# Products of ones ahead of the data, a first weight unit in halves, the first norm's squares on ScalarE and TensorE, and the last weight unit by token tile, in a two-layer mixer encoder

## The chip, the cores and the metric

The kernel runs as one program on one core of a Trainium2 chip. The metric is the device time of one execution in microseconds (us). Engines go by their names in the profile: PE is TensorE (PEld its weight loads), ACT is ScalarE, DVE is VectorE, POOL is GpSimd, and SP is SyncE, whose queue issues most DMA transfers.

## The reference, cut to what matters

Two layers run over 256 tokens of 2048 features. Each layer normalizes the tokens, multiplies them by one wide input matrix, feeds the parts to three mixers (a chunked mLSTM, a latent attention "MLA" and a dilated attention), projects back, and adds a feed-forward block of width 8192. All data are fp32.

```python
def rms_norm(x, gain):
    x32 = x.astype(jnp.float32)
    y = x32 * lax.rsqrt(jnp.mean(x32 * x32, axis=-1, keepdims=True) + EPS)
    return (y * gain.astype(jnp.float32)).astype(x.dtype)

def hybrid_layer(x, ...):
    h = rms_norm(x, norm_mix)
    z = jnp.einsum('bsd,de->bse', h, w_in)
    (ml_q, ml_k, ml_v, ml_o, ml_g, mla_cq, mla_ckv, dil_q, dil_k, dil_v) = jnp.split(z, ...)
    y_a = mlstm_mixer(...)      # 4 heads
    y_b = mla_mixer(...)        # 6 heads, on the normed latents c_q (384) and c_kv (128)
    y_c = dilated_mixer(...)    # 6 heads
    y = jnp.concatenate([y_a, y_b, y_c], axis=-1)
    x = x + jnp.einsum('bse,ed->bsd', y, w_out)
    h = rms_norm(x, norm_ff)
    u = jax.nn.relu(jnp.einsum('bsd,df->bsf', h, w_ff1))
    return x + jnp.einsum('bsf,fd->bsd', u * u, w_ff2)
```

The mean square of a token is one number per token, so the kernel multiplies the unnormed tokens (times the gain) by the matrix and scales the product by the root factor afterwards.

## The kernel before

**Numbers in two parts.** Every fp32 operand of a large product is split into a rounded part (`hi`, type fp32r) and the remainder (`lo`). One product of 128 features becomes three PE products: hi by hi, hi by lo, lo by hi (`token_group`, L383). The hi part is a copy on ACT, the lo part a subtraction on DVE.

**Weight units.** The weights come in 732 units of up to 128x1024 (512 KB), in the order in which PE uses them (`weight_order`, L260). `Weights.load` (L224) issues the transfer of a unit into one of 3 staging tiles `wst`; `Weights.split` (L231) makes `whi` on ACT and `wlo` on DVE, 4 tiles of each; `Weights.next` (L248) splits the unit two ahead of the one that PE takes and then issues one more load, which waits on SP's queue until the `wlo` of three units before has freed its staging tile.

**Groups.** The input matrix is done in 9 groups. A group is 8 units, and a unit is two feature tiles by two token tiles by three products, 12 products in all, that accumulate in two PSUM banks `g` (pool `gps`, 4 banks, so a third group needs the banks of the first). Below, group 0 is the first (latents, 512 columns), group 1 the second (336 columns: rope key, gates, part of the dilated values), group 2 the third (512 columns), in which after its fourth unit the first MLA head is started (hook `mla0`, L1028); their units are u0 to u7. In the profile's rows `g<-whi,xg` and `g<-wlo,xg` are these products, `xg` the tokens.

**The first tokens.** They come transposed as eight tiles `xt`, two feature tiles each. `first_xg` (L336) makes the hi part on ACT and the lo part on DVE, and for the first norm POOL squares each 128x256 piece (`sq`) and adds it to `acc`. When group 0 is done, `token_factor` (L433) sums `acc` over the partitions by two small fp32 products with a matrix of 1/2048 (`stat`), and the root factor `rt` comes from it through ACT and DVE. `latents` (L488) waits for `rt`, squares group 0's banks on ACT, computes its own factors, and scales the banks into `lat` with four ACT operations; only then are the two banks free.

**What sets the order.** Side work runs as generators (`Stream`, L117). At every product PE's planned clock advances, and a step of side work is written into the program when its due time on that clock has come. The order on each engine is fixed by this plan when the program is built; an engine runs its instructions strictly in that order.

**The end.** After the last product of the last group, `ff2_end` (L1124) adds the two banks to the tokens on DVE, one token tile after the other, and issues a transfer of each to `out` from ACT's queue.

## Time and profile before

| what | us |
|---|---|
| three runs | 2154.41, 2157.25, 2159.11 (median 2157.25) |
| profiled execution | 2155.49, its span 2153.3 |
| PE busy in the span | 2119.8 (98%) |
| DVE, ACT, POOL busy | 1322.4 (61%), 1082.3 (50%), 110.4 (5%) |

The profile follows the profiled execution. The span runs from the first to the last instruction, and 2.2 us lie around it. PE is the engine that sets the pace: over most of the span its products follow one another without a wait, and the time that is lost lies at the start, in the stretch of the mixers of each layer, and behind the last product. A row of the timeline gives start, duration, engine, line, operation, output and inputs, and in brackets how long the engine sat idle before it and what released it. The granted clock of PE has two levels, 1.00 (2.4 GHz) and 0.50 (1.2 GHz).

### The profile page before, as it was taken

To read this page: it belongs to the slowest core of one execution; us is meant where nothing else is said; L and a number is where in the kernel's file an instruction comes from. 1 tells how busy PE (TensorE), PEld (TensorE's weight loads), DVE (VectorE), ACT (ScalarE), POOL (GpSimd) and SP (SyncE) were. 2 spreads that over 40 slices of the span, in tenths; PEclk is the share of its full clock that TensorE was granted. 3 is DMA by queue.
4 is the path that set the end of the run, shared out by engine and by line. 5 is a ranking of instruction groups with operands and counts; after the bars stand their busy time and mean duration, and the time that the engine had idled before them with its cause. 6 is when DMAs were issued, how large, how long until landed. Compare 5 with 4: busy or idle time off the path is not lost.

```text
span 2153.3 us, 28894 instructions
## 1 busy us (share of the span) xinstructions
PE 2119.8 (98%) x10848; PEld 1804.9 (84%) x10848; DVE 1322.4 (61%) x1963; ACT 1082.3 (50%) x1883; POOL 110.4 (5%) x142
## 2 busy tenths in 40 slices
PE   8999999999999999999999999999999999999999
PEld 6788888888888888888887888888888888888887
DVE  7668755655564565565557687556546655655654
ACT  5666655543453444454456676554434434534442
POOL 6112100000000000000001121000000000000000
PEclk9999999999999999999999999999999999999999
DMA  7544455566656666566554444556565666566565
GB/s 228 189 141 126 154 175 181 187 194 190 193 186 195 194 188 193 190 192 196 178 174 142 143 128 153 174 189 192 186 198 189 190 191 195 187 195 194 187 200 162
DMA packets 109004, 389.89 MB, mean 181 GB/s; under 512 B 12352, under 2 KB 12480, under 8 KB 108608
## 3 DMA queue, kind: packets, MB, share of 16 engines
q1 hardware_dynamic: 107136, 384.97, 56.6%
q10 hardware_dynamic: 1728, 3.07, 0.4%
q8 instruction: 85, 1.39, 0.3%
q14 instruction: 55, 0.45, 0.1%
HBM read 385.90 MB, written 2.10 MB: 180 GB/s over the span
## 4 chain that ended last, share of the span: by engine, by line
PE 89%; ACT 4%; DVE 3%; POOL 2%; issue 1%; DMA 1%; POOLq 0%; ACTq 0%; DVEq 0%; SPq 0%
PE g L194 84%; ACT junk L98 1%; PE mla_z L194 1%; ACT whi L98 1%; DVE wlo L98 1%; POOL acc L98 1%; PE oT L194 1%; POOL sq L98 1%; DMA wst<-w_in 1%; PE xT L200 0%; PE pT L200 0%; PE dil_s L194 0%; PE mla_s L194 0%; POOL rp L98 0%; ACT dil_z L98 0%
## 5 line engine op out<-in xcount | busy, mean ns | idle before, releaser
L98 DVE TENSOR_TENSOR wlo<-wst,whi 128x1024 fp32r<-128x1024 f32 (+2 forms) x732 | 889.5, 1224 | 317.4 <-ACT whi L98 307.7
L98 ACT CAST whi<-wst 128x1024 fp32r<-128x1024 f32 (+2 forms) x732 | 761.2, 1043 | 539.7 <-PE g L194 402.5
L194 PE MATMUL g<-whi,u 128*128 128x512 f32 x2048 | 633.4, 389 | 0.0
L194 PE MATMUL g<-xg,whi 128*128 128x512 f32 x2048 | 489.8, 391 | 0.0
L194 PEld LDWEIGHTS g<-whi,u 128*128 128x128 f32 x2048 | 384.5, 188 | 79.6
L194 PEld LDWEIGHTS g<-xg,whi 128*128 128x128 f32 x2048 | 376.4, 188 | 72.8
L194 PE MATMUL g<-wlo,u 128*128 128x512 f32 x1024 | 398.4, 389 | 0.0
L194 PE MATMUL g<-whi,xg 128*128 128x512 f32 (+1 forms) x1152 | 371.7, 389 | 6.3 <-ACT whi L98 6.3
L194 PEld LDWEIGHTS g<-xg,wlo 128*128 128x128 f32 x2048 | 263.1, 191 | 12.1 <-ACT xg L98 2.0
L194 PE MATMUL g<-xg,wlo 128*128 128x256 f32 x2048 | 267.4, 283 | 1.1 <-ACT xg L98 1.1
L194 PEld LDWEIGHTS g<-whi,xg 128*128 128x128 f32 x1152 | 215.5, 189 | 44.0 <-ACT whi L98 6.3
L194 PEld LDWEIGHTS g<-wlo,u 128*128 128x128 f32 x1024 | 192.3, 188 | 39.8
L194 PE MATMUL g<-wlo,xg 128*128 128x512 f32 (+1 forms) x576 | 222.0, 385 | 3.3 <-DVE wlo L98 3.3
L98 ACT COPY ev<-g 128x256 f32<-128x256 f32 x128 | 48.0, 375 | 340.7 <-PE g L194 340.7
L98 DVE TENSOR_TENSOR ev<-g,ev 128x256 f32<-128x256 f32 x128 | 54.4, 425 | 229.8 <-ACT ev L98 229.7
L194 PE MATMUL g<-whi,y 128*128 128x512 f32 x512 | 162.8, 393 | 0.0
L194 PEld LDWEIGHTS g<-wlo,xg 128*128 128x128 f32 x576 | 109.1, 189 | 23.3 <-DVE wlo L98 6.7
L194 PEld LDWEIGHTS g<-whi,y 128*128 128x128 f32 x512 | 96.1, 188 | 19.7
L194 PE MATMUL g<-wlo,y 128*128 128x512 f32 x256 | 99.7, 389 | 0.0
L98 DVE SCALAR_TENSOR_TENSOR x<-g,r,x 128x512 f32<-128x512 f32 x64 | 45.8, 751 | 83.2 <-PE g L194 83.2
L98 DVE SCALAR_TENSOR_TENSOR ev<-ev 128x256 f32<-128x256 f32 x128 | 54.4, 425 | 4.4
L194 PEld LDWEIGHTS g<-wlo,y 128*128 128x128 f32 x256 | 48.1, 188 | 9.5
(206 smaller groups left out, 1199.1 us busy)
## 6 DMA issues: line engine op xcount, KB each, us to landing
wst<-w_ff SPq DMA_DIRECT2D x512, 512.0 KB, 4.2
wst<-w_in SPq DMA_DIRECT2D x128, 512.0 KB, 3.7
wst<-w_out SPq DMA_DIRECT2D x64, 512.0 KB, 4.2
wst<-w_in SPq DMA_DIRECT2D x16, 336.0 KB, 3.0
wst<-w_mla SPq DMA_DIRECT2D x12, 416.0 KB, 3.1
xt<-xT SPq DMA_DIRECT2D x8, 256.0 KB, 5.1
x<-x SPq DMA_DIRECT2D x2, 1024.0 KB, 7.1
out<-x ACTq DMA_DIRECT2D x8, 256.0 KB, 2.2
```

The costliest lines, as they stand in the source:

```text
L98: return fn(*args, **kw)
L194: c.nc.tensor.matmul(out, lhsT, rhs, start=start, stop=stop)
```

## The change

Four edits, the first three at the program's start.

1. `warm_up` writes a tile of ones on DVE and lets PE multiply it with itself 20 times (fp32, 128 columns) before anything else; the result is not used.
2. The first weight unit is loaded and split in two halves of 512 columns, and the first token tile is loaded from ACT's queue, so that SP's queue begins with the two halves.
3. POOL no longer squares. `first_squares` squares both feature tiles of one `xt` on ACT (128x512), and four fp32 products with two columns of the 1/2048 matrix add the sums to two PSUM banks `stat`, one of each token tile. The first four tiles are squared in the last four units of group 0, the other four in the first four units of group 1, and `token_factor` waits until the last is done.
4. `last_unit` does the very last unit of the last group with the token tile as the outer loop.

```diff
+WARM = 20
@@ class Weights
-        c.nc.sync.dma_start(self.st[self.d][:, :n], src)
+        for cols in self.pieces(self.d):
+            c.nc.sync.dma_start(self.st[self.d][:, cols], src[:, cols])
...
+    def pieces(self, i):
+
+        n = self.srcs[i][1]
+        return [slice(0, n // 2), slice(n // 2, n)] if i == 0 else [slice(0, n)]
...
-            nc.scalar.copy(hi[:, :n], st[:, :n])
+            for cols in pieces:
+                nc.scalar.copy(hi[:, cols], st[:, cols])
             yield
-            nc.vector.tensor_tensor(out=lo[:, :n], in0=st[:, :n], in1=hi[:, :n].bitcast(F32), op=ALU.subtract)
+            for cols in pieces:
+                nc.vector.tensor_tensor(out=lo[:, cols], in0=st[:, cols], in1=hi[:, cols].bitcast(F32),
+                                        op=ALU.subtract)
@@ def first_xg
-    if kt == 0:
-        c.acc = c.small.tile([P, S], F32, tag="acc", name="acc", bufs=1)
-        nc.gpsimd.tensor_tensor(out=c.acc, in0=src, in1=src, op=ALU.mult)
-    else:
-        sq = c.tmp.tile([P, S], F32, tag="sq", name="sq", bufs=1)
-        nc.gpsimd.tensor_tensor(out=sq, in0=src, in1=src, op=ALU.mult)
-        nc.gpsimd.tensor_tensor(out=c.acc, in0=c.acc, in1=sq, op=ALU.add)
-    c.s.cur.last.pop("pool", None)
...
+def first_squares(c, i, xt):
+
+    sq = c.tmp.tile([P, NT, S], F32, tag="sq", name="sq", bufs=1)
+    c.nc.scalar.activation(sq, xt, AF.Square)
+    yield
+    for j in range(2):
+        kt = 2 * i + j
+        for tt in range(NT):
+            mm(c, c.stat[tt][:, :2], sq[:, j, tt * P:(tt + 1) * P], c.mean[:, :2], kt == 0, kt == KT - 1)
...
+def last_unit(c, acts, ps, w):
+
+    hi, lo = c.w.next()
+    for tt in range(NT):
+        for j in range(2):
+            kt = KT - 2 + j
+            wh, wl = hi[:, j * w:(j + 1) * w], lo[:, j * w:(j + 1) * w]
+            xh = acts[kt][:, tt * P:(tt + 1) * P]
+            xl = acts[kt][:, S + tt * P:S + (tt + 1) * P]
+            mm(c, ps[tt], xh, wh, False, False)
+            mm(c, ps[tt], xh, wl, False, False)
+            mm(c, ps[tt], xl, wh, False, j == 1)
+            c.s.pump()
@@ def token_factor
-        ps = yield from bank(c, "stat")
+        while c.squares:
+            yield
         for tt in range(NT):
-            mm(c, ps[:, 2 * tt:2 * tt + 2], c.acc[:, tt * P:(tt + 1) * P], c.mean[:, :2], True, True)
-        yield
-        nc.vector.tensor_scalar(out=v, in0=ps[:, 0:4:2], scalar1=EPS, scalar2=None, op0=ALU.add)
-        c.s.give(m=1)
+            nc.vector.tensor_scalar(out=v[:, tt:tt + 1], in0=c.stat[tt][:, 0:1], scalar1=EPS, scalar2=None,
+                                    op0=ALU.add)
+        c.s.give(m=2)
...
+def warm_up(c):
+
+    ones = c.tmp.tile([P, P], F32, tag="sq", name="ones", bufs=1)
+    c.nc.vector.memset(ones, 1.0)
+    ps = new_bank(c, "warm")
+    for _ in range(WARM):
+        c.nc.tensor.matmul(ps[:, :P], ones, ones, start=True, stop=True)
@@ def mixers
-    ps = in_group(c, G1_W)
+    ps = in_group(c, G1_W, prepare=prepare1)
@@ def ffn
-            token_group(c, us, ps, 512)
+            if last_layer and ch == NCHUNK - 1 and g == NX - 1:
+                token_group(c, us, ps, 512, range(KT // 2 - 1))
+                last_unit(c, us, ps, 512)
+            else:
+                token_group(c, us, ps, 512)
@@ def encoder
+        if kp == 4:
+            c.stat = [new_bank(c, "stat") for _ in range(NT)]
+            c.s.take_now(m=2)
+        if kp >= 4:
+            c.s.step(c.s.spawn(first_squares(c, kp - 4, xts[kp - 4])))
...
+    def prepare1(kp):
+        if kp < 4:
+            t = c.s.spawn(first_squares(c, kp + 4, xts[kp + 4]))
+            c.s.step(t)
+            if kp == 3:
+                c.s.finish(t)
+                c.squares = False
...
-    for i in range(c.B_ST):
+    load_x(nc.scalar)
+    c.w.load()
+    for i in range(c.B_ST - 1):
         load_x()
         c.w.load()
     load_x()
+    c.squares = True
```

On PE, from the end of unit 4 of group 0 into unit 5, before (with buffer numbers: `g_170` and `g_171` are the banks of the two token tiles, `whi_267` and `wlo_268` unit 5):

```order
L194 MATMUL g_171<-wlo_237,xg_201 128x512
L194 MATMUL g_171<-whi_236,xg_201 128x512
L194 MATMUL g_170<-whi_267,xg_223 128x512
L194 MATMUL g_170<-wlo_268,xg_223 128x512
L194 MATMUL g_170<-whi_267,xg_223 128x512
L194 MATMUL g_171<-whi_267,xg_223 128x512
L194 MATMUL g_171<-wlo_268,xg_223 128x512
L194 MATMUL g_171<-whi_267,xg_223 128x512
L194 MATMUL g_170<-whi_267,xg_228 128x512
```

And the same place on PE now, where `sq` holds the squares, `const` the matrix of 1/2048, and `stat_279` and `stat_280` the sums of the two token tiles:

```order
L199 MATMUL g_180<-wlo_228,xg_201 128x512
L199 MATMUL g_180<-whi_227,xg_201 128x512
L199 MATMUL stat_279<-const_115,sq_281 128x2
L199 MATMUL stat_280<-const_115,sq_281 128x2
L199 MATMUL stat_279<-const_115,sq_281 128x2
L199 MATMUL stat_280<-const_115,sq_281 128x2
L199 MATMUL g_179<-whi_252,xg_220 128x512
L199 MATMUL g_179<-wlo_253,xg_220 128x512
L199 MATMUL g_179<-whi_252,xg_220 128x512
L199 MATMUL g_180<-whi_252,xg_220 128x512
L199 MATMUL g_180<-wlo_253,xg_220 128x512
L199 MATMUL g_180<-whi_252,xg_220 128x512
```

Eight such sets of four stand in the program, four in group 0 and four in group 1, the last at the end of the third unit of group 1; before, two `stat` products stood behind the third product of group 1.

On ACT, at the end of group 1, before (`lat` are group 0's banks scaled, which frees them; `z` takes group 1's first columns and so needs its last product):

```order
L98 ACTIVATE rs_a<-lat_ss 128x4
L98 ACTIVATE rs_y_476<-rs_a 128x4
L98 CAST whi<-wst 128x672
L98 ACTIVATE lat<-g,lat_f 128x384
L98 ACTIVATE lat<-g,lat_f 128x128
L98 ACTIVATE lat<-g,lat_f 128x384
L98 ACTIVATE lat<-g,lat_f 128x128
L98 CAST whi<-wst 128x672
L98 CAST whi<-wst 128x1024
L98 ACTIVATE lat_hl<-latT,vec 128x256 x2
L98 CAST whi<-wst 128x1024
L98 ACTIVATE z_583<-g,rt 128x80 x2
```

And the same place on ACT now:

```order
L99 ACTIVATE rs_a<-lat_ss 128x4
L99 ACTIVATE rs_y_549<-rs_a 128x4
L99 CAST whi<-wst 128x1024
L99 ACTIVATE z_595<-g,rt 128x80 x2
L99 CAST whi<-wst 128x1024
L99 ACTIVATE junk,kr_ss<-z_595 128x64 x2
L99 ACTIVATE lat<-g,lat_f 128x384
L99 ACTIVATE lat<-g,lat_f 128x128
L99 ACTIVATE lat<-g,lat_f 128x384
L99 ACTIVATE lat<-g,lat_f 128x128
L99 ACTIVATE dv<-g,rt 128x256 x2
```

The four `lat` have moved from ahead of `z` to behind `z`, a cast and `junk`.

On PE, where group 1 ends and group 2 begins, with the engines that each row waits for, before:

```order
L194 MATMUL g<-whi,xg 128x336
L194 MATMUL g<-whi,xg 128x512 [waits Activation_49]
L194 MATMUL g<-wlo,xg 128x512 [waits DVE_49]
L194 MATMUL g<-whi,xg 128x512
L200 MATMUL latT<-const,lat 128x128 x4
L194 MATMUL g<-whi,xg 128x512 [waits PE_49]
```

And now:

```order
L199 MATMUL g<-whi,xg 128x336
L199 MATMUL g<-whi,xg 128x512 [waits PE_49,Activation_49]
L199 MATMUL g<-wlo,xg 128x512 [waits DVE_49]
L199 MATMUL g<-whi,xg 128x512
L199 MATMUL g<-whi,xg 128x512 [waits PE_49,Activation_49]
```

The first product of each token tile of group 2 now waits for ACT, and both sets of `latT` stand further on in group 2.

## Rows read from the trace of the kernel before

**Rows 1.** Who waited for whom, 0 to 70 us: total, times, longest.

```profile
PE g L194 <- ACT whi L98: 6.3, 1, 6.3
PE g L194 <- DVE wlo L98: 2.7, 6, 0.8
PE ml_aT L200 <- DVE ml_na L98: 1.8, 1, 1.8
```

**Rows 2.** Timeline of PE, groups 0 and 1.

```profile
6.34 0.80 PE L194 MATMUL g<-whi,xg 128*128 128x512 f32 x1 [6.34 <-ACT whi L98]
7.83 0.79 PE L194 MATMUL g<-wlo,xg 128*128 128x512 f32 x1 [0.70 <-DVE wlo L98]
...
9.28 0.63 PE L194 MATMUL g<-wlo,xg 128*128 128x512 f32 x1
...
10.56 0.63 PE L194 MATMUL g<-wlo,xg 128*128 128x512 f32 x1
...
14.18 0.40 PE L194 MATMUL g<-wlo,xg 128*128 128x512 f32 x1
...
14.87 0.39 PE L194 MATMUL g<-wlo,xg 128*128 128x512 f32 x1
...
43.96 0.32 PE L194 MATMUL g<-wlo,xg 128*128 128x336 f32 x1
...
44.41 0.32 PE L194 MATMUL g<-wlo,xg 128*128 128x336 f32 x1
```

**Rows 3.** DVE's groups by form, 5 to 34 us: count, busy us, mean ns, idle before.

```profile
L98 DVE SCALAR_TENSOR_TENSOR xg<-xt,vec,xg 128x256 fp32r<-128x256 f32 x16 | 13.5, 886 | 4.6 <-ACT xg L98 4.6
L98 DVE TENSOR_TENSOR wlo<-wst,whi 128x1024 fp32r<-128x1024 f32 x8 | 13.3, 1671 | 0.1
```

**Rows 4.** DVE's groups by form, 45 to 100 us.

```profile
L98 DVE TENSOR_TENSOR wlo<-wst,whi 128x1024 fp32r<-128x1024 f32 x13 | 15.9, 1229 | 4.3 <-ACT whi L98 4.3
...
L98 DVE SCALAR_TENSOR_TENSOR lat_hl<-latT,vec,lat_hl 128x256 fp32r<-128x256 f32 x4 | 1.8, 480 | 3.8 <-ACT lat_hl L98 3.8
```

**Rows 5.** Stretches: length, busy of PE, PEld, DVE, ACT, POOL, PEclk, DMA, GB/s.

```profile
0.00:4.00 4.00, 0.00 (x0) 0.00 (x0) 0.00 (x0) 1.28 (x1) 0.31 (x5) 1.00 0.49 133
4.00:18.00 14.00, 10.96 (x36) 8.51 (x37) 13.28 (x14) 11.04 (x19) 12.98 (x15) 1.00 0.99 355
```

**Rows 6.** Timeline, the small fp32 products on PE and what follows them.

```profile
35.92 0.61 PE L194 MATMUL stat<-const,acc 128*128 128x2 f32 x4 [0.97 <-POOL acc L98]
...
36.38 0.40 PE L194 MATMUL g<-whi,xg 128*128 128x336 f32 x1
...
62.20 1.39 PE L194 MATMUL ml_F<-ml_lf,const 128*128 128x4 f32 x12
```

**Rows 7.** ACT's squares of 128x512: minimum, median, maximum ns.

```profile
L98 ACT ACTIVATE junk<-x x24: 621/632/635, 318.3 to 1443.6; 128x512 f32<-128x512 f32 x24
```

**Rows 8.** Timeline, from the scaling of group 0's banks into group 2.

```profile
43.94 1.57 ACT L98 ACTIVATE lat<-g,lat_f 128x384 f32<-128x384 f32 x4 [0.25 <-DVE lat_f L98]
...
50.87 0.79 ACT L98 ACTIVATE z<-g,rt 128x80 f32<-128x80 f32 x2
50.98 0.55 PE L194 MATMUL g<-whi,xg 128*128 128x336 f32 x2
...
52.04 0.50 PE L194 MATMUL g<-wlo,xg 128*128 128x512 f32 x1 [0.52 <-DVE wlo L98]
...
53.04 0.19 ACT L98 ACTIVATION_READ_ACCUMULATOR junk<-z 128x1 f32 x1
```

**Rows 9.** Timeline of PE at its longest wait behind the start.

```profile
101.83 1.17 PE L200 MATMUL pT<-const,sm_e 128*128 128x128 f32 x4 [2.46 <-DVE sm_e L98]
```

**Rows 10.** Stretches of 2 us around it, columns as in rows 5.

```profile
100.00:102.00 2.00, 0.17 (x1) 0.17 (x1) 1.91 (x6) 1.27 (x5) 0.00 (x0) 0.79 0.57 215
...
106.00:108.00 2.00, 2.00 (x11) 2.00 (x11) 1.21 (x2) 2.00 (x3) 0.00 (x0) 0.51 0.01 4
```

**Rows 11.** Timeline, DVE's last two additions.

```profile
2148.61 1.43 DVE L98 SCALAR_TENSOR_TENSOR x<-g,r,x 128x512 f32<-128x512 f32 x2 [7.89 <-PE g L194]
```

More of the change, by code (lines that the diff above doesn't have):

```diff
@@ L146, in give, with take_now @@
             self.room[k] += v
+    def take_now(self, **n):
+        self.until(lambda: all(self.room[k] >= v for k, v in n.items()))
+        self.give(**{k: -v for k, v in n.items()})
     def spawn(self, gen):
@@ L227, in load @@
         self.st[self.d] = c.wp.tile([P, 1024], F32, tag="wst", name="wst", bufs=c.B_ST)
-        c.nc.sync.dma_start(self.st[self.d][:, :n], src)
+        for cols in self.pieces(self.d):
+            c.nc.sync.dma_start(self.st[self.d][:, cols], src[:, cols])
         self.d += 1
+    def pieces(self, i):
+        n = self.srcs[i][1]
+        return [slice(0, n // 2), slice(n // 2, n)] if i == 0 else [slice(0, n)]
     def split(self):
         c, nc = self.c, self.c.nc
-        st, n = self.st.pop(self.k), self.srcs[self.k][1]
+        st, pieces = self.st.pop(self.k), self.pieces(self.k)
         hi = c.wp.tile([P, 1024], F32R, tag="whi", name="whi", bufs=c.B_HL)
@@ L999, in ml_head, with mixers @@
     c.s.give(m=1, t2=1, half=1)
-def mixers(c, prepare, after):
+def mixers(c, prepare, prepare1, after):
     nc, s = c.nc, c.s
@@ L1168, in encoder @@
     c.w = Weights(c, weight_order(c, depth))
+    warm_up(c)
     rest = load_vectors(c, 0)
@@ L1175, in encoder, with load_x @@
     state = dict(x=0, xg=0)
-    def load_x():
+    def load_x(queue=nc.sync):
         xts.append(tile2k(c, "xt", F32).rearrange("p (i s) -> p i s", i=2))
-        nc.sync.dma_start(xts[-1], xT[:, 2 * state["x"]:2 * state["x"] + 2])
+        queue.dma_start(xts[-1], xT[:, 2 * state["x"]:2 * state["x"] + 2])
         state["x"] += 1
@@ L1221, in encoder @@
     for l in range(depth):
-        mixers(c, prepare if l == 0 else None, load_tokens if l == 0 else None)
+        mixers(c, *((prepare, prepare1, load_tokens) if l == 0 else (None, None, None)))
         out_proj(c)
```

## The prediction

> **What bounds the kernel now.** I read the busy shares first: PE has 98%, so over most of the 2153.3 us only fewer or faster products help, and all four edits lie in the first 55 us or in the last two. There the list of waits is read next [rows 1]: PE stood 6.3 us before its first product, 2.7 us in six waits for `wlo`, and 1.8 us at `ml_aT` in group 2. Then PE's timeline [rows 2]: the first product starts at 6.34, the second at 7.83; from 9.28 to 10.56 three products take 1.28 us, 0.43 each, and from 14.18 to 14.87 three take 0.69, 0.23 each. So the first dozen ran at the lower level, 1.2 GHz, and the later ones at 2.4 GHz; the column of the granted clock says 1.00 there, the spacing says otherwise. A product of 336 columns takes 0.15 (three in 0.45 from 43.96 to 44.41). Then DVE: while POOL squares, an `xg` lo part takes 886 ns and a `wlo` 1671 [rows 3]; later, with POOL mostly idle, the same kinds take 480 and 1229 [rows 4]. In group 0 DVE needs 2 x 0.89 + 1.67 = 3.4 us for a unit, PE only 12 x 0.23 = 2.8: DVE sets the pace there, and POOL's squares make it do so.
>
> Group 1 ends at 50.98 + 0.15 = 51.13 [rows 8]. Its and group 0's 192 products need 96 x 0.23 + 96 x 0.15 = 36.5 us. From 6.34 that leaves 51.13 - 6.34 - 36.5 = 8.3 us which are not products at full clock: the low clock, the waits for DVE, the wait for POOL's sum (0.97) with the two `stat` products (0.46) [rows 6], and one set of transposes. The change can take those 8.3 us and part of the 6.3 away.
>
> **Products of ones (added).** Twenty fp32 products of 128 columns have no row. The lower bound is a small fp32 product: two take 0.46 from 35.92 to 36.38, six `ml_F` at most 1.39 [rows 6], so 0.22 each and 4.4 in all. The upper bound is a product of 512 columns at 1.2 GHz, 0.43 [rows 2], since the kernel's own planner charges an fp32 product four times its columns: 8.6 in all. They can start at about 1.0 us (an estimate: ACT and POOL are at work well inside the first 4 us [rows 5], and DVE first writes the ones). PE then sees work without a break, as it did from 7.83 until the spacing fell between 10.56 and 14.18. I take 12 at 0.43 and 8 at 0.22, and PE is free for data at 1.0 + 6.9 = 7.9; the bounds give 5.4 and 9.6.
>
> **First unit in halves.** Half a cast and half a `wlo`, and DVE without POOL beside it, would let the first product start near 6.1 and the second near 6.9 instead of 6.34 and 7.83. By the value above PE is still at its ones, so this is worth nothing unless the ones end early; ones that end at 5.4 would leave 6.9 as the start that counts. The first token tile, moved to ACT's queue behind a small load of gains, shares the transfer engines with the halves, and unit 1 stands behind the same bytes as before.
>
> **Squares off POOL (removed), onto ACT and PE (added).** DVE drops to 2 x 0.48 + 1.23 = 2.2 us a unit, below PE's 2.8, and its waits in group 0 go. What is late next is the transfers: 768 KB a unit at 355 GB/s [rows 5] is 2.2 us, below 2.8 too. ACT gets eight squares of 0.63 [rows 7]; with two hi parts and a cast it stays under PE's pace, and that cover is not in danger, as the tiles are two units ahead. But each square waits for the `stat` set before it, as there is one `sq` tile, and the casts queue behind it on ACT. Only the last set feels that: it stands three products behind the one before it, and 0.63 for the square against 3 x 0.15 leaves about 0.3.
>
> PE gets 32 `stat` products, all on its path, as it has no waits left to hide them in. At 0.22 that is 7.0 us. The bounds are 0.15 each, where a two-column product would cost as little as one of 336 columns (4.8), and 0.23 (7.4); the nearest row is `stat` itself. The first set also needs `const`, now in use 14 us ahead of the old `stat` product. Before it in the queue go eight token tiles and seven units, with itself 6.5 MB: 0.53 by 4.0 us and the rest at 355 GB/s [rows 5] lands near 21.0 to 22, and PE reaches the set at 7.9 + 60 x 0.23 = 21.7. I charge 0.2, at most 1.5.
>
> End of group 1: 7.9 + 36.5 + 7.0 + 0.3 + 0.2 = 51.9, against 51.13: **+0.8**. The ones, the relief of DVE and the products of the squares cancel.
>
> **The root factor comes later (moved).** It was made at the start of group 1, and the latents' chain behind it ended with four `lat` from 43.94 to 45.51, long before group 2 [rows 8]. Now its last `stat` set ends with the third unit of group 1, five units or 9 us before the group's end. The chain needs as long as before, 45.51 - 36.38 = 9.1 us, and the plan has put `lat` on ACT behind `z`, a cast and `junk`. `z` needs the last products of group 1. Before, `z` began 0.26 ahead of the group's end and `junk` ended at 53.04 + 0.19 = 53.23, 2.36 later [rows 8]; so `lat` starts 2.1 behind the group's end, and its first pair takes 1.57 / 2 = 0.8. The first product of group 2 waits for that pair, the fourth for the second pair: 2.9 + 0.15 = 3.05 us in which PE stands. Before, PE lost 0.7 here (the second product at 52.04 where 51.36 was due). Net **+2.4**. Bounds: 1.3, if the cast's data were late already and `lat` not, and 4.5, if the cast waits for its transfer.
>
> Both sets of `latT` now stand in group 2, so one more is paid there that left group 1: four transposes, half of the 1.17 us that they take at the low clock [rows 9], **+0.5**. During the 3 us the weights and the token load run on, so the `wlo` that DVE had in front of `ml_na` is no longer late; of the 1.8 us at `ml_aT` [rows 1] the chain of three small DVE operations behind `ml_F` stays, some 0.6: **-1.2**, and a few tenths of waits for `wlo` in group 2 go, **-0.4**. Behind that the order on every engine is as before.
>
> **The last unit by token tile.** Before, both additions ended at 2148.61 + 1.43 = 2150.04 [rows 11], the second right after the last product. The first now runs under the last products, and the first transfer is off the queue sooner, but the second addition still starts with the last product's end: **-0.1**, at most -0.7.
>
> Sum: 0.8 + 2.4 + 0.5 - 1.2 - 0.4 - 0.1 = **+2.0**. On the profiled execution, 2155.5 (span 2153.3 and 2.2 around it), that is 2157.5. The median of the three runs is 1.8 above that execution, and the forecast is put there: 2157.25 + 2.0, **2159.3**.
>
> **The rivals.**
>
> *The wait before group 2 costs the clock as well (slower).* At 101.83 PE had stood 2.46 us [rows 9]; the granted clock fell in that stretch (0.79 from 100 to 102) and was still low from 106 to 108 (0.51) [rows 10]. The new wait is longer, 3.05 us. The Trainium skill (TensorE: Matmul & The Clock Gate, What's actually happening) has the lower rate as the default, which only activity lifts; by that rule the stand ahead of group 2 gives back what the products of ones bought, and rows 9 and 10 agree with it. Against it: the wait of 1.8 us at `ml_aT` cost no clock, so it depends on where the wait falls. Four to seven us of group 2 at half rate cost 2 to 3.4, so 2161.3 to 2162.7; with ones that end at 9.6 instead of 7.9, 2163 to 2164.4. It decides from about 4.6 us at low clock.
>
> *The squares cost PE little (faster).* If the weight loads of the two-column products hid behind the 512-column products beside them, a set would cost 0.2 instead of 0.9, 5.5 less, and the factor would be there earlier, so that 1 us of the wait ahead of group 2 went too: 2152.8. Against it: the `stat` and `ml_F` rows stood among the same products and took 0.22 each. With ones that end early it would be 2151.5.
>
> *The ones do not lift the clock (slower).* PE would be free at 9.6 and run 2.7 us of data at half rate, 1.35 lost: 9.6 + 1.35 instead of 7.9, +3: 2162.4. For it only that no row shows such products.
>
> **How the numbers follow.** No change within 0.2%, which is 4.3 us and about what a measurement of this kernel can tell, spans 2152.9 to 2161.6. The forecast, with a clock that falls for a short while or not at all, has 0.60. The low clock ahead of group 2 has 0.22, ones that do not lift it 0.05, the cheap squares 0.13. So faster 0.13, same 0.60, slower 0.27. The range takes in the bounds of the forecast (`stat` at 0.15 each: -2.2; the ones at 5.4, so a start at 6.9: -1.0; the wait at 4.5: +1.5; the ones at 9.6: +1.7) and the likelier half of the slow rival: 2153.5 to 2163.5. The forecast's own range is 2156 to 2161.5.
>
> **What would show it.** Right: 20 `warm` products from about 1 to 8 us, spacing 0.43 and then 0.22; the first `g` product at full clock; `wlo` near 1.2 us in group 0 and no wait for it; `stat` sets of 0.9 us; group 1 ending near 52; then PE idle some 3 us, released by ACT's `lat`; `ml_aT` waiting under 1 us. Wrong: a wait ahead of group 2 under 1.5 us, sets under 0.5 us, or a second stall of PE in group 0 by transfers.

## The result, and the profile after

| | us |
|---|---|
| changed kernel | median 2169.99 (2167.82 to 2172.45, four runs) |
| kernel before, same chip | median 2156.54 (2154.41 to 2159.11, four runs) |
| ratio, 95% interval | 1.0062 (1.0045 to 1.0080) |
| profiled execution after | 2171.66, span 2169.8 (before 2155.49, span 2153.3) |

The change makes the kernel slower by 13.4 us, 0.6%. The forecast was 2159.3 and its range ended at 2163.5: it was wrong.

PE's waits up to 90 us in the changed kernel (total, times, longest), against [rows 1]:

```profile
PE g L199 <- ACT lat L99: 2.7, 1, 2.7
PE stat L199 <- DMA const<-const: 2.4, 1, 2.4
PE g L199 <- DVE wlo L99: 2.1, 1, 2.1
PE warm L495 <- DVE ones L99: 1.1, 1, 1.1
PE ml_aT L205 <- DVE ml_na L99: 0.6, 1, 0.6
PE stat L199 <- ACT sq L99: 0.2, 1, 0.2
```

The six small waits for `wlo` and the wait for the first weights are gone. Three single waits of 2.1 to 2.7 us stand in their place. DVE's groups by form from 5 to 34 us show DVE freed once POOL no longer squares beside it, against 1671 and 886 ns in [rows 3]:

```profile
L99 DVE TENSOR_TENSOR wlo<-wst,whi 128x1024 fp32r<-128x1024 f32 x7 | 8.7, 1236 | 5.9 <-ACT whi L99 5.9
L99 DVE SCALAR_TENSOR_TENSOR xg<-xt,vec,xg 128x256 fp32r<-128x256 f32 x16 | 6.9, 478 | 5.3 <-ACT xg L99 5.3
```

PE's timeline at the prediction's steps, against [rows 2, 6, 8]:

```profile
1.05 6.68 PE L495 MATMUL warm<-ones 128*128 128x128 f32 x40 [1.05 <-DVE ones L99]
7.49 0.47 PE L199 MATMUL g<-whi,xg 128*128 128x512 f32 x1
...
24.23 1.02 PE L199 MATMUL stat<-const,sq 128*128 128x2 f32 x8 [2.38 <-DMA const<-const]
...
43.52 0.95 PE L199 MATMUL stat<-const,sq 128*128 128x2 f32 x8
44.32 0.40 PE L199 MATMUL g<-whi,xg 128*128 128x336 f32 x1
...
62.63 0.51 PE L199 MATMUL g<-whi,xg 128*128 128x512 f32 x1 [2.70 <-ACT lat L99]
...
75.48 0.50 PE L199 MATMUL g<-wlo,xg 128*128 128x512 f32 x1 [2.08 <-DVE wlo L99]
...
82.40 0.38 PE L205 MATMUL ml_aT<-const,ml_na 128*64 128x128 f32 x2 [0.60 <-DVE ml_na L99]
```

Each `stat` set of four fp32 products (two rows each, so x8) takes 44.32 - 43.52 = 0.80 us at full clock. In the stretches below (columns as in [rows 5]) the granted clock is third from the end:

```profile
26.00:32.00 6.00, 6.00 (x19) 5.02 (x18) 2.18 (x2) 2.29 (x3) 4.60 (x13) 0.50 0.34 108
50.00:52.00 2.00, 2.00 (x9) 2.00 (x8) 1.42 (x7) 1.63 (x6) 0.00 (x0) 0.50 0.45 143
64.00:66.00 2.00, 2.00 (x6) 1.56 (x5) 1.79 (x4) 1.29 (x4) 0.00 (x0) 0.50 0.98 381
78.00:80.00 2.00, 2.00 (x6) 1.57 (x5) 1.17 (x3) 0.98 (x3) 1.48 (x3) 0.50 0.90 336
84.00:86.00 2.00, 2.00 (x11) 2.00 (x11) 1.66 (x4) 1.76 (x6) 0.00 (x0) 0.50 0.00 0
```

These are five stretches at 1.2 GHz ahead of 100 us: 25.65 to 32.48, 49.54 to 52.96, 63.20 to 66.61, 76.85 to 80.26 and 83.67 to 87.09, 20.5 us in all. Products take twice as long there, so half of it, about 10 us, is my estimate of what they cost. Behind its first products the kernel before has none there; both have the one at `pT` (101.14 to 107.97 before, 117.81 to 124.64 after). From `mla_z` on, which starts at 82.54 against 67.26, the two traces run alike, some 16 us apart. (This execution is 1.7 us above the median, and over the four the mean granted clock was 0.992 in the two longer and 0.994 in the two shorter ones, so the low stretches vary between executions.)

Why a `wlo` was late at 75.48 is read on DVE, which takes its instructions in order:

```profile
70.66 0.88 DVE L99 SCALAR_TENSOR_TENSOR lat_hl<-latT,vec,lat_hl 128x256 fp32r<-128x256 f32 x2 [4.87 <-ACT lat_hl L99]
71.46 0.17 DVE L99 TENSOR_SCALAR ml_t<-ml_t 128x16 f32<-128x16 f32 x1
...
74.21 2.15 DVE L99 TENSOR_TENSOR wlo<-wst,whi 128x1024 fp32r<-128x1024 f32 x2
```

`lat_hl` waited for ACT, which waited for the `latT` products that now stand in group 2; fourteen small operations of the gates and then `wlo` stood behind it. At the end of the program:

```profile
2164.56 0.75 DVE L99 SCALAR_TENSOR_TENSOR x<-g,r,x 128x512 f32<-128x512 f32 x1 [7.21 <-PE g L199]
...
2165.49 0.39 PE L199 MATMUL g<-whi,u 128*128 128x512 f32 x1
2165.92 0.75 DVE L99 SCALAR_TENSOR_TENSOR x<-g,r,x 128x512 f32<-128x512 f32 x1 [0.61 <-PE g L199]
```

The first addition is now over when the last product starts (2164.56 + 0.75 = 2165.31); before, it started 0.25 us ahead of the last product's start (2148.61 [rows 11] and 2148.86). The second still follows the last product. From its end to the end of the span are 3.1 us now and 3.2 before.

### The profile page after: what moved, and what is told of

The parts are those of the page before. It is cut to its first block, busy times and chain, and to the rows that moved or that the text cites. A ratio compares the mean times of both kernels' runs of the same rounds, so it can differ in the third digit from the quotient of the medians.

```text
span 2169.8 us, 29079 instructions
## 1 busy us (share of the span) xinstructions
PE 2139.6 (99%) x10948; PEld 1824.3 (84%) x10948; DVE 1312.0 (60%) x1966; ACT 1088.0 (50%) x1892; POOL 80.5 (4%) x111
## 4 chain that ended last, share of the span: by engine, by line
PE 91%; ACT 4%; DVE 3%; issue 1%; DMA 1%; POOL 1%; SPq 0%; POOLq 0%; ACTq 0%; DVEq 0%
PE g L199 85%; PE mla_z L199 1%; ACT junk L99 1%; ACT whi L99 1%; DVE wlo L99 1%; PE oT L199 1%; PE xT L205 0%; PE mla_s L199 0%; PE pT L205 0%; PE dil_s L199 0%; DMA const<-const 0%; DMA wst<-w_in 0%; PE stat L199 0%; POOL rp L99 0%; ACT dil_z L99 0%
## 5 line engine op out<-in xcount | busy, mean ns | idle before, releaser
L99 DVE TENSOR_TENSOR wlo<-wst,whi 128x1024 fp32r<-128x1024 f32 (+3 forms) x733 | 885.7, 1217 | 331.6 <-ACT whi L99 321.9
L99 ACT CAST whi<-wst 128x1024 fp32r<-128x1024 f32 (+3 forms) x733 | 761.7, 1042 | 522.5 <-PE g L199 401.7
L199 PE MATMUL g<-whi,xg 128*128 128x512 f32 (+1 forms) x1152 | 377.5, 393 | 2.7 <-ACT lat L99 2.7
```

The lines of the kernel that those rows point to most:

```text
L99: return fn(*args, **kw)
L199: c.nc.tensor.matmul(out, lhsT, rhs, start=start, stop=stop)
```

## The experiments

Times are medians; the difference is to the kernel before, run beside it on the same chip (2156.1 to 2157.2). The intervals reach some 0.1% (2 us) or more to either side, so a step of under some 2 us between two rows (3 where a kernel ran only four times) is not clear of noise by the times alone; where the text goes by such a step, it says what the traces show.

| kernel | us | difference | ratio, 95% interval |
|---|---|---|---|
| before + ones | 2160.78 | +3.9 | 1.0020 (1.0010 to 1.0030) |
| before + ones in their own tile | 2158.01 | +1.9 | 1.0010 (1.0001 to 1.0020) |
| after without the squares' move | 2161.19 | +4.3 | 1.0022 (1.0012 to 1.0031) |
| squares' move alone | 2165.98 | +9.1 | 1.0047 (1.0030 to 1.0063) |
| after, `const` wait filled | 2169.67 | +12.6 | 1.0054 (1.0040 to 1.0068) |
| after, own mean tile | 2165.65 | +8.8 | 1.0041 (1.0026 to 1.0056) |
| ... and `lat` ahead of `z` | 2163.24 | +7.2 | 1.0031 (1.0019 to 1.0043) |
| mean tile and early factor | 2161.27 | +5.2 | 1.0022 (1.0012 to 1.0032) |
| ... and half the sets | 2152.92 | -4.2 | 0.9981 (0.9972 to 0.9991) |
| ... all sets, rows of x later | 2160.32 | +3.2 | 1.0012 (1.0003 to 1.0021) |
| squares summed on DVE | 2153.40 | -2.7 | 0.9989 (0.9980 to 0.9998) |
| ... `const` later | 2151.67 | -5.4 | 0.9973 (0.9963 to 0.9984) |
| ... `const` later, no ones | 2152.06 | -5.0 | 0.9974 (0.9964 to 0.9983) |
| ... `const` and rows of x later | 2154.37 | -2.8 | 0.9990 (0.9981 to 0.9999) |
| ... the same, no ones | 2156.95 | -0.2 | 0.9999 (0.9990 to 1.0007) |
| ... `const` later, rows of x in parts | 2149.69 | -7.2 | 0.9968 (0.9956 to 0.9979) |
| ... the same, no ones | 2151.15 | -5.8 | 0.9974 (0.9964 to 0.9984) |

**The ones alone**, in the kernel before:

```diff
+WARM = 20
...
+def warm_up(c):
...
+    warm_up(c)
     rest = load_vectors(c, 0)
```

> The kernel before plus the forty products of ones alone; squares stay on POOL, weight units whole, last unit as before. Theory A (the change loses its time on the squares: the wait for const, the two-column products and the clock that falls after them; DVE paces group 0 as long as POOL squares beside it): the clock is up by about 5.3 us instead of 12.39, the waits of g for wlo in group 0 grow by what the products gain, and the time stays within 1 us of before. Rival B (the ones are worth what the prediction gave them, whatever squares the first norm): 2.4 to 3 us faster than before. Rival C (the ones themselves bring the low clock at 25.65): low clock near 25 us here too, 3 us slower or more.

Measured +3.9, outside both A and B. The number is C's, but C's low clock at 25 us was not there. POOL's timeline and PE's show an effect of the edit that I had not seen:

```profile
8.19 0.78 POOL L99 TENSOR_TENSOR sq<-xt 128x256 f32<-128x256 f32 x1 [3.41 <-PE warm L464]
```

```profile
38.70 1.01 PE L195 MATMUL stat<-const,acc 128*128 128x2 f32 x4 [4.66 <-POOL acc L99]
```

The ones live in the tile `sq`, so POOL's second square waited until PE had read them; the clock then was low from 36.7 to 43.5. In the changed kernel POOL squares nothing, so this cannot be its loss. Repeated with a tile of their own:

```diff
-    ones = c.tmp.tile([P, P], F32, tag="sq", name="ones", bufs=1)
+    ones = c.cp.tile([P, P], F32, tag="ones", name="ones", bufs=1)
```

> The kernel before plus the forty products of ones, which now have a tile of their own and no longer hold the tile that POOL's first square writes (in the first run of the ones alone POOL waited 3.41 us for them, its sum came 2.8 us later and PE waited 4.66 us for it). Theory F (POOL's chain of squares and sums sets the start of group 1, and the ones did harm only through the shared tile): POOL's sum is there at 35.9 us as before, PE waits for it longer than the 0.97 us of before (up to 3 us), the time is 2155 to 2158, the same as before. Rival G (a longer wait of PE for that sum lowers the clock in group 1 whatever its cause): sum at 35.9, low clock between 36 and 45 us, 2158.5 to 2161.

+1.9: 2158.01 lies at the upper end of F's range, and the low clock between 36 and 45 us that G has did not come. The last sum on POOL and the product that needs it, in this run:

```profile
35.32 0.72 POOL L99 TENSOR_TENSOR acc<-acc,sq 128x256 f32<-128x256 f32 x1
```

```profile
36.10 0.61 PE L195 MATMUL stat<-const,acc 128*128 128x2 f32 x4 [0.96 <-POOL acc L99]
```

against 35.92 in [rows 6]. PE's wait for the sum did not grow, as F had it: what the ones gained went into waits for `wlo` ahead of it (3.0 us up to 45 us, 2.2 before). While POOL squares and sums, DVE beside it and POOL's last sum set the start of group 1, and a faster start of PE buys nothing.

**Everything but the squares' move:**

```diff
@@ first_xg
+        nc.gpsimd.tensor_tensor(out=sq, in0=src, in1=src, op=ALU.mult)
+        nc.gpsimd.tensor_tensor(out=c.acc, in0=c.acc, in1=sq, op=ALU.add)
...
@@ prepare
-            c.s.step(c.s.spawn(first_squares(c, kp - 4, xts[kp - 4])))
...
```

> The changed kernel with the first norm's squares back on POOL and their sum multiplied by PE at once as before; ones, halves, x from ACT's queue and the last unit by token tile kept. Theory A: group 0 is paced by DVE beside POOL again, no low clock between 5.3 and 100 us, the time within 1.5 us of before (2155 to 2157.5). Rival B: 2.4 us or more faster than before. Rival E (halves, queue or last unit carry part of the loss): 3 us or more slower than before.

+4.3, by its number E. But PE waited 3.2 us for POOL's sum, whose second square had waited 1.67 us for the shared tile again, and the clock was low from 39.72 to 43.13, so the run does not price the halves, the queue and the last unit.

**The squares' move alone:**

```diff
-    warm_up(c)
...
-        return [slice(0, n // 2), slice(n // 2, n)] if i == 0 else [slice(0, n)]
+        return [slice(0, n // 2), slice(n // 2, n)] if False else [slice(0, n)]
...
-            if last_layer and ch == NCHUNK - 1 and g == NX - 1:
+            if False:
...
-    load_x(nc.scalar)
-    c.w.load()
-    for i in range(c.B_ST - 1):
+    for i in range(c.B_ST):
```

> The changed kernel without the ones, without the halves, x's second tile on SP's queue and with the old last unit: only the first norm's squares on ACT and PE. Theory A (the squares cost all of the loss): 7 to 16 us slower than before, with low clock in one or more stretches between 24 and 90 us that before does not have; the first product of stat waits for const only if it comes before 24 us, which without the ones it does by 1 us at most. Rival C (the ones are at fault for the low clock): 4 to 6 us slower than before (stat products 6.7 us and the later factor, less DVE's relief), clock as before until 100 us.

+9.1, low clock at 56.6 to 60.0 and 70.3 to 73.7: A. The squares' move alone costs 9.1 of the 13.4. PE comes to the first `stat` set at 23.37 here and waits for nothing; in the change it comes at 21.85 (24.23 - 2.38) and waits for `const`. The next runs price that wait.

**The wait for `const`.** First removed, by two columns that DVE sets:

```diff
+    c.tiny = c.cp.tile([P, 2], F32, tag="tiny", name="tiny", bufs=1)
+    c.nc.vector.memset(c.tiny, 1.0 / D)
...
-  mm(c, c.stat[tt][:, :2], sq[...], c.mean[:, :2], kt == 0, kt == KT - 1)
+  mm(c, c.stat[tt][:, :2], sq[...], c.tiny, kt == 0, kt == KT - 1)
```

> The changed kernel with the two columns of 1/2048 from a tile that DVE sets, so that the first stat products wait for no transfer; the rest as in the change. Theory A (the wait for const, 2.38 us, sets off the low clock at 25.65 to 32.48): the wait is gone and that stretch runs at full clock: 2.4 us plus about half of 6.8 us less than after, 2163 to 2165. Rival D (the two-column products lower the clock by themselves, wait or no wait): low clock at about the same place, 1.5 to 2.5 us less than after, 2167.5 to 2168.5.

4.7 us less than the change (13.45 to 8.79), nearest to A, and about what the squares' move alone costs. The same two-column sets ran, and the stretch that was low is at full clock:

```profile
26.00:32.00 6.00, 6.00 (x33) 5.04 (x32) 3.10 (x3) 3.50 (x5) 6.00 (x14) 1.00 0.53 154
```

Then filled instead of removed:

```diff
     yield
+    if i == 0:
+        ps = new_bank(c, "fill")
+        for _ in range(24):
+            c.nc.tensor.matmul(ps[:, :P], c.ones, c.ones, start=True, stop=True)
...
-    ones = c.tmp.tile([P, P], F32, tag="sq", name="ones", bufs=1)
+    ones = c.ones = c.cp.tile([P, P], F32, tag="ones", name="ones", bufs=1)
```

> The changed kernel with 24 products of ones just ahead of the first stat products, so that PE multiplies while const is on its way; it waits for nothing for about 2.7 us less. It tells the wait from the low clock that follows it. Theory A (the idle time sets off the low clock at 25.65 to 32.48): that stretch is at full clock, the time 2 to 4 us less than after, 2166 to 2168. Rival D (products of two columns lower the clock by themselves): low clock from about 25.7 as in after, 2169.5 to 2171.

```profile
21.43 5.52 PE L369 MATMUL fill<-ones 128*128 128x128 f32 x48
26.79 0.95 PE L199 MATMUL stat<-const,sq 128*128 128x2 f32 x8
```

I had priced a product at half of what it takes, so the set came 2.56 us later than in the change. The stretch from 26 to 32 ran at full clock here as well. The total is only 0.9 less than the change's, which the noise covers, and outside A's range because of the overlong fill. The traces tell more: the set came 2.56 us later, yet group 2 began 0.71 us earlier (61.92 against 62.63), so the low clock behind the wait cost about 3.3 us in the change. In this run and the one before the same narrow products ran and PE did not stand: there the idle time took the clock away, not these products.

**The late factor.** ACT scales `lat` ahead of `z`:

```diff
@@ latents, behind the four lat operations
+    c.lat_read = True
...
@@ mixers
+    c.lat_read = False
     lat = s.spawn(latents(c, ps, rt, tf))
...
+    s.until(lambda: c.lat_read)
     z1 = c.cp.tile([P, NT, MLA_ROPE + 16], F32, tag="z1", name="z1", bufs=1)
```

> The run with the mean tile, and ACT scales lat ahead of z, so that the banks of group 2 are free sooner. Theory A: the wait of 2.7 us ahead of group 2 shrinks to under 1.2 us, the low clock at 56 to 62 us goes with it, 3 to 6 us less than with the mean tile alone: 2160 to 2163. Rival H (the late factor keeps its price, since the same chain is only cut at another place: what is queued behind lat on ACT and DVE comes later): less than 1.5 us gained, 2164 to 2166.

1.6 less by the differences, 2.4 by the medians: between the two, although the wait ahead of group 2 and its low clock did go. What was queued behind came later, and the clock fell there (low from 68.82 to 75.65):

```profile
69.05 0.61 PE L205 MATMUL ml_aT<-const,ml_na 128*64 128x128 f32 x2 [2.72 <-DVE ml_na L99]
...
71.73 0.44 PE L205 MATMUL ml_At<-const,ml_A 64*128 64x64 f32 x2 [1.23 <-DVE ml_A L99]
```

Then the factor from group 0's four sets alone, with the other four still multiplied:

```diff
-  ... kt == 0, kt == KT - 1)
+  ... kt % 8 == 0, kt % 8 == 7)
+    if i == 3:
+        c.squares = False
...
```

> The run with the mean tile, but the first norm's factor is made from the first eight of the sixteen row blocks alone, right after group 0; the other 16 products are still run in group 1 and their sums are left unused, so the output is another. It prices the late factor apart from the products. Theory A (the late factor costs the wait ahead of group 2, the low clock behind it and the wait for wlo at 69.8): these three go, 6 to 8 us less than with the mean tile, 2157 to 2160; the products' 6 us remain. Rival J (the products themselves carry it): 2163 to 2165.

3.6 less, between A and J. The wait ahead of group 2 went; PE waited 4.07 us at `ml_aT` instead.

**Half the sets.** The last four sets and their squares are left out as well:

```diff
@@ prepare1
-            t = c.s.spawn(first_squares(c, kp + 4, xts[kp + 4]))
-            c.s.step(t)
...
```

> The run with the early factor and without the last four of the eight sets of products and their squares (the output is another): it prices 16 of the 32 products. Theory A (a set costs PE 0.81 us): 3.2 us less than the run with the early factor, 2157 to 2159. Rival K (the sets also cost by the low clock at 70 to 77 us): that goes too, 2153 to 2156.

9.4 less, K and more, for sixteen products whose own time is 3.2 us and their four squares on ACT. The two runs at `ml_aT`, first with all sets, then with half:

```profile
71.27 0.60 PE L205 MATMUL ml_aT<-const,ml_na 128*64 128x128 f32 x2 [4.07 <-DVE ml_na L99]
```

```profile
63.14 0.41 PE L205 MATMUL ml_aT<-const,ml_na 128*64 128x128 f32 x2 [0.90 <-DVE ml_na L99]
```

With all sets the clock was low from 70.0 to 76.8, with half not at all there. The traces add it up, the clock by an estimate: 3.2 of products, 3.2 of waiting at `ml_aT` (4.07 against 0.90), 0.8 of waiting for a square at 43.23 and 3.4, half of the low stretch, less 0.6 of waiting for a `wlo` that only half the sets have, are 9.9 of the 10.5 us between the two profiled executions. What held `ml_na` is on DVE, a `wlo` whose cast waited 7.57 us on ACT for its weights, in a stretch in which the transfers were full (all sets):

```profile
69.32 1.23 DVE L99 TENSOR_TENSOR wlo<-wst,whi 128x1024 fp32r<-128x1024 f32 x1 [4.60 <-ACT whi L99]
70.46 0.17 DVE L99 COPY ml_Fs<-ml_F 128x16 f32<-128x16 f32 x1
```

```profile
68.24 1.04 ACT L99 CAST whi<-wst 128x1024 fp32r<-128x1024 f32 x1 [7.57 <-DMA wst<-w_in]
```

```profile
58.00:68.00 10.00, 9.05 (x45) 7.07 (x43) 6.20 (x22) 1.83 (x4) 1.34 (x3) 1.00 0.98 382
```

The 2 MB of x's rows (`load_tokens`, issued behind group 1) stand in SP's queue ahead of these weights. Moving them ahead of group 4 tests that:

```diff
     s.spawn(ml_gates(c, z1))
-    if after:
-        after()
...
     s.spawn(ml_v(c, ps, rt))
+    if after:
+        after()
```

> The run with the early factor and all 32 products (the last 16 sums unused, the output another), with x's rows issued ahead of group 4. Theory L: the wait of 4.07 us for ml_na and the low clock at 70 to 77 us go, so that only the products' own time is left against the run with half the sets: 4 to 7 us less than with the rows ahead of group 2, 2154 to 2157.5. Rival M: 2160 to 2162.

The wait at `ml_aT` went from 4.07 to nothing and `mla_z` started 5.6 us earlier, as L has it, yet the total fell by 2.0 only: at 140.84 PE waited 3.15 us for `sm_e`, behind a stretch from 128 to 138 us in which rows and weights filled the transfers (share 0.98), and the clock was low from 141.33 to 144.74. In the time this is M's number by L's mechanism.

**The squares kept off POOL and off PE.** ACT squares, DVE adds the tiles inside group 0, four products at its end:

```diff
+def first_squares(c, i, xt):
+    if i == 0:
+        c.acc = tile2k(c, "acc", F32)...
+        c.nc.scalar.activation(c.acc, xt, AF.Square)
+        ...
+    c.nc.scalar.activation(sq, xt, AF.Square)
+    yield
+    c.nc.vector.tensor_tensor(out=c.acc, in0=c.acc, in1=sq, op=ALU.add)
...
```

> The changed kernel with the squares on ACT but summed by DVE in pairs of 512 columns, all inside group 0, so that PE multiplies one sum by four short products at the end of group 0, as early as the kernel before. Theory A (the price lies in the 32 products, the late factor and the clock, not in squares on ACT): group 0 ends 4 to 6 us earlier than in before, no low clock between 5.3 and 90 us, 2149 to 2153. Rival I (in group 0 something else paces when POOL is gone, DVE with its seven sums or the weights' transfers): 2154 to 2158, and PE waits for wlo or whi in group 0.

-2.7, by what it shows rival I. ACT waited 1.72 us for weights (to 19.91) and 1.35 for tokens (to 22.30) while `const` and `vecs` were under way, and the one `sq` tile made ACT and DVE wait in turn (0.7 to 2.0 us each time). PE stood 1.01 us for `whi` at 26.11 and 1.10 for `wlo` at 27.70, the clock fell at 27.38, and `stat` came at 35.15. Mended:

```diff
-        if kp == 2:
+        if kp == 5:
             nc.sync.dma_start(c.const, const[:, :C_ALL])
...
-    sq = c.tmp.tile([P, NT, S], F32, tag="sq", name="sq", bufs=1)
+    sq = tile2k(c, "sq", F32)...
...
+    c.tiny = c.cp.tile([P, 2], F32, tag="tiny", name="tiny", bufs=1)
...
-WARM = 20
+WARM = 15
```

> The run with the sum on DVE, mended where its trace showed new waits: the const and vecs transfers are issued three units later (they stood ahead of the weights that whi waited for at 26.1 us), each square has a buffer of its own, the columns of 1/2048 come from a tile that DVE sets, and 15 ones products in place of 20. Theory A (nothing paces group 0 but PE then): group 0 ends at 29.5 to 31 us against 35.92 in before, no low clock between 5.3 and 95 us, 2149 to 2152.5. Rival I (weights' transfers or DVE pace it all the same): ends at 33 us or later, 2153 to 2156.

-5.4, theory A by its time and by the end of group 0. The clock was still low from 62.48 to 65.89, which A had excluded, behind a wait of 2.00 us at `ml_aT`. `stat` now stands at 30.27, against 35.92 in [rows 6]:

```profile
30.27 0.95 PE L199 MATMUL stat<-tiny,acc 128*128 128x2 f32 x8
```

The products of ones removed from it:

```diff
-    for _ in range(WARM):
+    for _ in range(0):
```

> The same without the products of ones: their price where POOL's sum no longer sets the start of group 1. Theory A: the first six units' products run at low clock to 12.4 us as in before, 1.5 to 3 us slower than with the ones. Rival: the same time within 0.7 us, as the ones alone gave in the kernel before.

0.4 slower, the rival's answer: `stat` came 2.0 us later, but `ml_aT` without a wait, where the run with the ones stood 2.00 us; the clock was low for 3.4 us in both, from 60.36 here. x's rows issued ahead of group 4, as above, in both:

> The run with the sum on DVE and const later, and the two transfers of x's rows (1 MB each, needed only by the output projection) issued ahead of group 4 in place of ahead of group 2. Theory L (from the issue of these rows at 47.65 us on, the transfers are full and the weights behind them, whi at 58.8 us after 5.74 us of waiting, hold DVE's queue and by it ml_aT, which comes 13.4 to 14.2 us after that issue in every run): the wait of 2.0 us for ml_na and the low clock at 62 to 66 us go, 2 to 5 us less: 2147 to 2150. Rival M (DVE's own chain holds ml_na): the wait stays within 0.7 us of 2.0, the time within 1 us of 2151.7.

> The same without the products of ones. Theory L: with the transfers out of the way what PE gains at the start is kept, so the ones are now worth 1.5 to 2.5 us: 2149 to 2152. Rival M: the two runs stay within 0.7 us of one another, as they did with the rows' transfer ahead of group 2.

The wait for `ml_na` and the low clock at 62 to 66 went, as L has it, and the median rose by 2.6 all the same, outside both ranges. (L's distance of 13.4 to 14.2 us from the issue of the rows to `ml_aT` does not hold in every run: it is 14.6 with the early factor and 23.4 in the change.) Where the 2.6 lie the traces cannot show, as the two profiled executions took 2153.30 and 2153.42. This one has the transfers full from 125 to 135 us and a new wait behind them:

```profile
125.00:135.00 10.00, 9.52 (x48) 7.63 (x46) 5.76 (x15) 3.97 (x8) 1.34 (x3) 1.00 1.00 392
```

```profile
136.78 0.72 PE L205 MATMUL pT<-const,sm_e 128*128 128x128 f32 x4 [2.26 <-DVE sm_e L99]
```

The ones were worth 2.6 us in this pair. Then the rows in four pairs of transfers of 512 columns (256 KB each), at the first and the fifth unit of groups 6 and 7:

```diff
+        ps = in_group(c, 512, hooks(5 + pair), prepare=after if pair else None)
...
+    def load_tokens(kp):
+        if kp % 4 == 0:
+            part = next(parts)
             for tt in range(NT):
-                nc.sync.dma_start(c.x[tt], x[tt])
+                nc.sync.dma_start(c.x[tt][:, part], x[tt, :, part])
```

> The run with the sum on DVE and const later, and x's rows in four pairs of transfers of 256 KB, one ahead of every fourth unit of groups 6 and 7, where the run with the rows ahead of group 4 shows shares of 0.25 to 0.6. That run lost ml_na's wait, its low clock and 1.6 us up to 97 us, but the transfers were full from 125 to 135 us and a wait of 2.26 us for sm_e followed at 136.8. Theory L (any stretch where rows and weights together fill the transfers becomes a wait of PE): neither wait is left, 2147 to 2150.5. Rival M (the waits wander whatever the rows do): 2151 to 2155.

> The same without the products of ones. Theory L: what the ones gain at the start is kept, they are worth 1.5 to 2.5 us. Rival M: within 0.7 us of the run with the ones.

-7.2, inside L's range, and neither wait is left, though the clock still was low from 59.43 to 62.84. The stretch that was full:

```profile
125.00:135.00 10.00, 10.00 (x55) 8.29 (x53) 7.44 (x17) 5.82 (x16) 2.23 (x3) 1.00 0.61 207
```

The ones bring 1.5 here, about as much as the noise. This version beats both kernels: 2149.69, ratio 0.9968 (0.9956 to 0.9979) to before. That it also beats the rows in one piece behind group 1 (2151.67) is near the noise by the times; the traces show the wait of 2.00 us gone.

## Why the prediction was wrong

Right were the mechanisms and sizes in the first 20 us (free for data at 7.9, measured 7.49, at full clock; DVE's relief), the time at which PE comes to the first set (21.7 forecast, 21.85 measured), a `stat` set (0.88 forecast, 0.80 measured at full clock), the wait ahead of group 2 (3.05 forecast; group 1 ended at 59.76, the next product came at 62.63, so 2.87), the chain in front of `ml_aT` (0.6) and the last unit (-0.1).

**The largest term that the sum lacks is the clock: "a clock that falls for a short while or not at all" stands in it at nothing.** It fell five times ahead of 100 us, and half of those 20.5 us is about 10 us by estimate. The profiled executions lie 16.2 us apart, 14.2 more than the forecast of +2.0.

**The step that failed first is "I charge 0.2, at most 1.5" for `const`.** It was 2.38. The rate in that step held: 357 GB/s from 4.0 to 24.2 us against 355. The bytes did not: 7.2 MB moved in that time, and the step counts 6.0 (6.5 less the 0.53 of the first 4 us). It leaves out `vecs`, 468 KB that ACT's queue issued at 14.11, and what SP's queue issued behind `const`; `const` was issued at 16.27 and landed near 24.2. And the wait had a second price that the step did not ask for, the low clock from 25.65 to 32.48. Together they cost 4.7 us by the run with the mean tile. The end of group 1, forecast at 51.9, came at 59.76: of the 7.9 between, 2.2 are this wait and, by estimate, 3.4 and 1.7 are half of the two low stretches.

**"The wait before group 2 costs the clock as well" was made a rival with 0.22, for one place.** It came true there (63.20 to 66.61), and behind the waits for `const` (25.65) and for `wlo` (76.85) too; the falls at 49.54 and 83.67 had no such wait in front. The Trainium skill (TensorE: Matmul & The Clock Gate, What's actually happening), cited for it, says that the low rate is the default and activity lifts it; the filled wait agrees, with the clock at 1.00 from 26 to 32 us where the change has 0.50. I had taken one wait that cost no clock, 1.8 us [rows 1], as ground for 0.60 on the other side.

**"Behind that the order on every engine is as before" was wrong in what it was used for.** The order was kept, but `latT` moved into group 2, and with it DVE's chain. The 1.2 that the prediction took off at `ml_aT` came true (1.8 to 0.6). The 0.4 that it took off for waits for `wlo` in group 2 did not: PE stood 2.08 us for one at 75.48, which had no term.

**The sum took the 32 products at their own time, 7.0.** Eight sets at full clock are 6.4 (7.4 as they ran, since one fell into the first low stretch). But in the pair of runs that leaves out the sixteen in group 1 and their squares, these cost 9.4: their own 3.2, and the waits and the low clock that followed. The prediction treated what PE loses ahead of group 2 as a plain sum; in that pair the stretch behind it was held by x's rows and the weights. In the change itself it was held by DVE's chain behind `latT`, as `ml_aT` waited 0.60 us only.

**Nor did the ones and the halves gain what they gave PE.** They brought it to the first set 1.5 us sooner than the squares' move alone (21.85 against 23.37), and the wait for `const` took that and more. With that wait gone, the change with the mean tile (+8.8) and the squares' move alone (+9.1), which has neither ones, halves, queue nor last unit, are level within the noise. In the kernel before, DVE and POOL's sum hid such a gain. With the sum on DVE the ones were worth 0.4, 2.6 and 1.5 us in three pairs of runs; these versions are 0.2 to 7.2 us faster than before.

What stays open: why the clock fell at 49.54 (at 48.34 in the run with the filled wait), as PE had stood 0.21 us only, and at 83.67. The narrow products are not cleared there, though sets of the same shape at 42 to 44 us in the squares' move alone brought no fall. Nor was the share of halves, queue and last unit measured by itself.

## What to carry to other kernels

Work moved onto the engine that sets the pace is priced by where it stands as well as by its own time: it delays what is chained behind it, and a wait of about 2 us took the clock for several more in some places here and not in others. Before a chain is sped up at its start, look for the engine that ends last at its next meeting point: PE's wait for POOL's sum was under 1 us, yet group 0 ended 5.65 us sooner (30.27 against 35.92) in the version with the ones and without POOL. When a transfer's landing is forecast, count the bytes of every queue. A large transfer that nobody needs soon can be issued in parts where the transfers have room; here that took away the waits that it caused in one piece.

## What the runs showed of the hardware that was not expected

PE's clock fell in places where PE had hardly stood. In the run with `const` later and no ones, PE was busy from 58 to 62 us; it fell at 60.36, behind six fp32 products of four columns (twelve rows of the trace), with a wait of 0.61 us some way ahead of them, at 57.52:

```profile
58.00:60.00 2.00, 2.00 (x17) 1.81 (x15) 1.09 (x5) 0.37 (x1) 0.66 (x2) 1.00 0.79 229
60.00:62.00 2.00, 2.00 (x7) 1.65 (x7) 1.29 (x2) 1.08 (x2) 0.66 (x2) 0.59 0.85 336
```

In the two runs with x's rows in parts it fell behind the same products (59.43 and 59.73). In the two with the rows ahead of group 4 these products stood at 59.21 and 59.12, behind waits of 0.95 and 0.61, and the clock stayed at 1.00.

And a wait's length alone did not tell. At `ml_aT` a wait of 2.00 us was followed by low clock in the run with `const` later; waits of 2.01 in the run with the ones' own tile, 2.02 in the first run with the sum on DVE and 2.31 in the change without the squares' move were not:

```profile
61.82 0.38 PE L205 MATMUL ml_aT<-const,ml_na 128*64 128x128 f32 x2 [2.00 <-DVE ml_na L99]
```

```profile
67.39 0.38 PE L201 MATMUL ml_aT<-const,ml_na 128*64 128x128 f32 x2 [2.01 <-DVE ml_na L99]
```

```profile
71.75 0.38 PE L205 MATMUL ml_aT<-const,ml_na 128*64 128x128 f32 x2 [2.31 <-DVE ml_na L99]
```

Nor did the place: the wait of 2.08 us for the same `wlo` in group 2 was followed by low clock in the change (76.85) and in the squares' move alone (70.26), and not in the run with the mean tile:

```profile
69.81 0.50 PE L199 MATMUL g<-wlo,xg 128*128 128x512 f32 x1 [2.08 <-DVE wlo L99]
```
